# HGRN2 scores: two chunks in one product, half of the scores transposed

## The chip, the cores and the metric

The kernel runs on one core of one Trainium2 chip. The number that counts is the device time in microseconds of one execution, as the median of several. Inside the core, TensorE multiplies matrices into PSUM, VectorE and ScalarE work on elements, GpSimd clears memory and issues some transfers, and SyncE (SP) issues most of the transfers between HBM and the on-chip memory SBUF.

## The reference, cut to what matters

One layer of a decoder trunk over 512 tokens and 1024 channels: a combined projection, four causal mixers side by side, a gated merge, an output projection and an MLP. The change is in mixer A, HGRN2, which has 4 heads with 128 key and 128 value channels:

```
diff = cum[:, :, :, None, :] - cum[:, :, None, :, :]
dec = jnp.exp(jnp.where(causal[:, :, None], diff, NEG_BIG))
a = jnp.einsum('bhtd,bhtsd,bhsd->bhts', q_, dec, k_)
o = (jnp.einsum('bhts,bhsv->bhtv', a, v_)
     + jnp.einsum('bhtd,bhdv->bhtv', q_ * jnp.exp(cum), S))
```

`cum` is the running sum of the log of the forget gate within a chunk. The score of query t and key s is a sum over 128 channels, each with its own decay between s and t. The decay stands inside the sum, so one plain product of queries and keys does not give it. Only s <= t counts.

## The kernel before

Chunks. The kernel takes chunks of 128 tokens, so a head has NCH = 4 chunks, and arrays have the 128 channels in the partitions and 512 tokens in the columns. `A` (tile name `hA`) holds the scores, 128 partitions (keys s) by 4 chunks of 128 columns (queries t).

Levels. A decay between s and t can be split at any point m between them, exp(cum[t] - cum[m]) times exp(cum[m] - cum[s]), and then the sum over channels is a plain product. The kernel does so by levels n = 1, 2, 4, ..., 64: at level n, tokens are cut into blocks of 2n, and the split point is the middle of each block. The scores of queries in a second half with keys in the first half of the same block come from that level. The diagonal comes from q times k, summed over channels by a product with ones. Level 1 is done in the same way (`p1`, `p1d`). For n from 2 on, `level(n)` makes a tile `g` (name `hG`) of 512 columns: decayed keys where a token is in a first half, decayed queries where it is in a second half.

Products. For n = 2, 4, 8, 16, each chunk of `g` is multiplied with itself, four 128x128 fp32 products into one PSUM tile (`hg`), and a predicated copy with mask `h{n}` takes the wanted squares into `A`. For n = 32 and 64, `g` is packed differently (keys of all chunks in one half, queries in the other), two products give everything wanted, and 4 or 2 small copies of n partitions take out the squares. After the levels the head makes `he`, `hqd`, `hkd`, transposes the decayed keys (`hkt`), and runs over the four chunks: scores times values, state times queries, new state (`ho`, `htb`, `hgS`).

Order of the work. Nothing is issued in the order of the source. Every call goes through a recorder (`_Flow`, `wrap`, line 223; matmuls at line 434, transposes at 475), which keeps its engine, a cost by formula, and what it depends on. VectorE's cost is 65 + 1.04 n ns for n elements a partition where a PSUM operand or two inputs are involved (line 214), a ScalarE operation costs 92 + 0.833 n from SBUF, a DMA of SyncE 500 ns. `lay_out` then runs a list schedule over five engines with these costs and writes the instructions of each engine in the resulting order; on the chip each engine follows its order and waits on semaphores. Two kinds of tasks are mixed. The stream is the sequence of the projections: weight loads of 1 MB (`raw`, on SP's queue), the split of each weight into a high and a low part (`whi` on ScalarE, `wlo` on VectorE), and three matmuls of 512 columns for each pair (`pf`, `pt`, `pbr`, `yo`, `dn`). The mixers' heads are the other tasks, up to five at once. On TensorE the stream has the lowest rank:

```
rank = (9 if eng == "pe" and not self.urgent else 0, i)
```

On the other engines it has the highest. The stream's order is: projections of the mixers, then four merges (branches 3, 0, 1, 2; attention is branch 2 and comes last), each in two halves of four gate units (`pf`) and four branch units (`pbr`), then the output projection (`yo`) and the MLP (`pf` from `h_hi`, and `dn`).

Constants are one array in HBM, loaded by `late_constants` into the tile `cm` by one DMA on SP's queue, after the first units are under way: masks `y32`, `y64` (used by mixer D too), `h1` to `h64`, and others.

At the end, the last output tile is scaled and added in two VectorE pieces of 256 columns, each written out by a DMA on SP's queue.

Of the kernel before, what the change touches and what calls it, by code (L numbers as in the profile page):

```python
# [20 lines left out]
P = 128  # L21
# [17 lines left out]
def shape_constants():  # L39
    cols = []  # L40
    pos = 0

    def put(name, a):
        nonlocal pos
        full = np.zeros((P, a.shape[1]), np.float32)
        full[: a.shape[0]] = a
        _OFF[name] = (pos, pos + a.shape[1])
        pos += a.shape[1]
        cols.append(full)

    i = np.arange(P)
    s, t = i[:, None], i[None, :]
    put("ident", np.eye(P))
    put("minc", np.where(t >= s, 0.0, NEG))
    put("mstr", np.where(t > s, 0.0, NEG))

    def first_to_second(a, b, n):
        return (a // (2 * n) == b // (2 * n)) & ((a // n) % 2 == 0) & ((b // n) % 2 == 1)

    for n in (32, 64):  # L60
        put(f"y{n}", (first_to_second(t, s, n)) * 1.0)
    for n in (1, 2, 4, 8, 16, 32, 64):
        put(f"h{n}", first_to_second(s, t, n) * 1.0)
    put("scan", np.tile((np.arange(T) % P != 0) * 1.0, (P, 1)))
    sgn = np.ones((P, 1))
    sgn[32:36] = -1.0
    sgn[64:68] = -1.0
    put("sgn", sgn)
    global NCONST
    NCONST = pos  # L70
    dist = 255 - np.arange(384)
    nf = np.maximum(dist, 16).astype(np.float32)
    large = 16 + (np.log(nf / np.float32(16)) / np.float32(math.log(8.0)) * np.float32(16)).astype(np.int32)
    bucket = np.where(dist < 16, dist, np.minimum(large, 31))
    ok = (dist >= 0) & (dist < 128)
    oneh = np.zeros((33, 384))
    for m in range(384):
        if ok[m]:
            oneh[bucket[m], m] = 1.0
        else:  # L80
            oneh[32, m] = NEG
    put("oneh", oneh)
    return np.concatenate(cols, 1).astype(np.float32)
# [6 lines left out]
class _Flow:  # L90
# [85 lines left out]
    def wrap(self, key, eng):  # L176
        flow = self

        class W:
            def __getattr__(self, name):  # L180
                fn = getattr(eng, name)

                def call(*a, **k):
                    ops = dict(k)
                    if "out" not in ops:
                        ops["out"], a = a[0], a[1:]
                        call_a = (ops["out"],) + a
                    else:
                        call_a = a
                    out = ops.pop("out")  # L190
                    outs = [out] + ([ops.pop("accum_out")] if "accum_out" in ops else [])
                    ins = [v for v in list(a) + list(ops.values()) if isinstance(v, bass.AP)]
                    n = 1
                    for d in out.shape[1:]:
                        n *= d
                    big = [v for v in ins if v.space == PSUM]
                    table, dma = None, 0
                    if name == "dma_start":
                        dma = n * out.shape[0] * 4
                        c = 1000 if key == "g" else 500 if key == "y" else 60  # L200
                    elif key == "v":
                        if name == "tensor_tensor_scan":
                            c = 65 + 2.09 * n
                        elif name == "reciprocal":
                            c = 65 + 6.26 * n
                        elif name in ("tensor_copy", "tensor_scalar", "memset") and not big:
                            c = 65 + 0.52 * n
                        elif name in ("reduce_sum", "reduce_max"):
                            m = 1
                            for d in ins[0].shape[1:]:  # L210
                                m *= d
                            c = 65 + 1.04 * m
                        else:
                            c = 65 + 1.04 * n
                        if name in ("tensor_scalar", "scalar_tensor_tensor") and len(ins) > (1 if name == "tensor_scalar" else 2):
                            c += 65
                    elif key == "s":
                        f = a[1] if name == "activation" and len(a) > 1 else k.get("func")
                        table = {AF.Exp: "e", AF.Ln: "e", AF.Sigmoid: "s", AF.Silu: "u"}.get(f)
                        c = (52 if big else 92) + 0.833 * n + 95 * ("accum_out" in k) + 93 * sum(isinstance(k.get(x), bass.AP) for x in ("scale", "bias"))  # L220
                    else:
                        c = 110 + n * (0.8 if name == "memset" else 2.15 if len(ins) > 1 else 1.0)
                    flow.record(key, c, lambda: fn(*call_a, **k), outs, ins, table, dma,  # L223
                                two="accum_out" in k)

                return call

        return W()
# [176 lines left out]
def tile_hybrid_parallel_gated_mixers(  # L405
# [96 lines left out]
    def con(name):  # L502
        a, b = _OFF[name]
        return cm[:, a:b]

    def con4(name):
        return con(name).unsqueeze(1).to_broadcast([P, NCH, P])
# [653 lines left out]
    def hg_head(h):  # L1161
# [14 lines left out]
        act(p1, p1, AF.Exp)  # L1176
        tt(p1, p1, two[1][:, :, 1], ALU.mult)
        tt(p1, p1, two[2][:, :, 0], ALU.mult)
        p1d = bcast("hd", onesr, parts("hp", p1), ps("hd", (P, 256)))
        V.copy_predicated(A.rearrange("p (c a u) -> p c a u", c=NCH, u=2)[:, :, :, 1],  # L1180
                          con("h1").bitcast(I32).rearrange("p (a u) -> p a u", u=2)[:, :, 1].unsqueeze(1)
                          .to_broadcast([P, NCH, 64]), p1d.rearrange("p (c a) -> p c a", c=NCH))

        def level(n):
            nb = T // (2 * n)

            def four(a):
                return a.rearrange("p (a u n) -> p a u n", u=2, n=n)

            cv = four(cum)  # L1190
            mid = cv[:, :, 0, n - 1:n].to_broadcast([P, nb, n])
            g = z2("hG")
            gv = four(g) if n < 32 else g.rearrange("p (u a n) -> p a u n", u=2, n=n)
            tt(gv[:, :, 0, :], mid, cv[:, :, 0, :], ALU.subtract)
            tt(gv[:, :, 1, :], cv[:, :, 1, :], mid, ALU.subtract)
            act(g, g, AF.Exp)
            tt(gv[:, :, 0, :], gv[:, :, 0, :], four(k)[:, :, 0, :], ALU.mult)
            tt(gv[:, :, 1, :], gv[:, :, 1, :], four(q)[:, :, 1, :], ALU.mult)
            return g

        for n in (2, 4, 8, 16, 32, 64):
            g = level(n)
            yield
            if n < 32:
                gp = bank4("hg", lambda c, o: mm(o, ch(g, c), ch(g, c)))
                V.copy_predicated(c3(A), con4(f"h{n}").bitcast(I32), c3(gp))
                continue

            gp = ps("hg", (P, 2, P))
            for i in range(2):  # L1210
                mm(gp[:, i, :], ch(g, i), ch(g, 2 + i))
            A5 = A.rearrange("p (i c t) -> p c i t", i=2, c=2)
            for b in range(P // n):
                cc, s0 = b // (64 // n), b % (64 // n) * 2 * n
                V.tensor_copy(A5[s0:s0 + n, cc, :, s0 + n:s0 + 2 * n], gp[b * n:(b + 1) * n, :, b * n:(b + 1) * n])
        e = z2("he")
        act(e, cum, AF.Exp)
        qd, kd = z2("hqd"), z2("hkd")
# [456 lines left out]
    def mlp_units():  # L1675

        for hf in range(NH):
# [11 lines left out]
            for j in range(2):  # L1689
                obox = {}  # L1690
                for kg in range(FH // 4):
                    r0 = (hf * FH + kg * 4) * P
                    subs = []
                    for k2 in range(2):
# [5 lines left out]
                        def step(k, c, kg=kg, k2=k2, box=box, obox=obox, hf=hf, j=j, ah=ah, al=al):  # L1700
                            kk = kg * 4 + k2 * 2 + k
                            if kk == 0 and c == 0:
                                obox["o"] = [ps("dn") for _ in range(4)]
                            o = obox["o"][c]
                            mm3(o, ch(ah[kk], c), ch(al[kk], c), box["hi"][:, k, :], box["lo"][:, k, :],
                                kk == 0, kk == FH - 1)
                            n = 2 if kk == FH - 1 and hf == NH - 1 and j == 1 and c == 3 else 1
                            for a in range(n if kk == FH - 1 else 0):
                                cs = slice(a * T // n, (a + 1) * T // n)
                                stt(acc[c][j][:, cs], o[:, cs], tail["rs2"][:, c:c + 1], acc[c][j][:, cs], ALU.mult, ALU.add)  # L1710
                                if hf == NH - 1:
                                    Y.dma_start(out[c * P:(c + 1) * P, j * T + cs.start:j * T + cs.stop], acc[c][j][:, cs])

                        order = [(k, c) for k in range(2) for c in range(4)]
                        if kg == FH // 4 - 1 and k2 == 1:
# [95 lines left out]
```

## Time and profile before

| | |
|---|---|
| median of 3 runs | 1097.21 us (1096.2 to 1097.26) |
| the profiled execution | 1096.43 us |
| its span on the core | 1094.6 us |
| TensorE busy | 1081.7 us, 99% |
| VectorE busy | 678.4 us, 62% |
| ScalarE busy | 535.6 us, 49% |
| granted TensorE clock, mean | 0.997 |

The span runs from the first to the last instruction in the profile; the execution's own time is 1.83 us longer. A matmul's bar ends by a model and overlaps with the next matmul's bar, so its price is read from start to start. PE is TensorE's matmuls, PEld its weight loads, DVE is VectorE, ACT is ScalarE, SPq is SyncE's queue. Almost every line of the trace is line 223, 434 or 475, the recorder's, so instructions are told apart by their tiles.

### The profile page before, as it was taken

To read this page: it belongs to the slowest core of one execution; us is meant where nothing else is said; L and a number is where in the kernel's file an instruction comes from. 1 tells how busy PE (TensorE), PEld (TensorE's weight loads), DVE (VectorE), ACT (ScalarE), POOL (GpSimd) and SP (SyncE) were. 2 spreads that over 40 slices of the span, in tenths; PEclk is the share of its full clock that TensorE was granted. 3 is DMA by queue.
4 is the path that set the end of the run, shared out by engine and by line. 5 is a ranking of instruction groups with operands and counts; after the bars stand their busy time and mean duration, and the time that the engine had idled before them with its cause. 6 is when DMAs were issued, how large, how long until landed. Compare 5 with 4: busy or idle time off the path is not lost.

```text
span 1094.6 us, 14138 instructions
## 1 busy us (share of the span) xinstructions
PE 1081.7 (99%) x5339; PEld 905.9 (83%) x5339; DVE 678.4 (62%) x1417; ACT 535.6 (49%) x970; POOL 30.2 (3%) x69
## 2 busy tenths in 40 slices
PE   8999999999999999999999999999999999999998
PEld 8889888898888888778887888888888888888886
DVE  5765999758999999976387334545443324444232
ACT  5764478226774778776267233345442222443220
POOL 4000000000000001000000010000000000000000
PEclk8999999999999999999999999999999999999999
DMA  6342554515422355222322252323232323232331
GB/s 235 89 107 97 157 182 153 185 49 167 142 87 87 108 170 174 78 78 78 116 78 77 83 186 91 102 77 116 77 116 77 116 77 116 78 115 80 113 116 39
DMA packets 95580, 122.19 MB, mean 112 GB/s; under 512 B 11104, under 2 KB 65844, under 8 KB 95256
## 3 DMA queue, kind: packets, MB, share of 16 engines
q1 hardware_dynamic: 90216, 115.03, 32.3%
q0 software_dynamic: 1984, 5.61, 1.6%
q10 hardware_dynamic: 3312, 0.66, 0.3%
q8 instruction: 42, 0.69, 0.3%
q14 instruction: 26, 0.21, 0.1%
HBM read 110.74 MB, written 12.11 MB: 112 GB/s over the span
## 4 chain that ended last, share of the span: by engine, by line
PE 79%; DVE 12%; ACT 5%; issue 2%; DMA 1%; SPq 0%; DVEq 0%; ACTq 0%
PE pf L434 41%; PE dn L434 16%; PE pbr L434 6%; PE yo L434 4%; PE pt L434 4%; DVE wlo L223 2%; DVE hG L223 2%; DVE hA L223 1%; ACT whi L223 1%; ACT L223 1%; ACT L400 1%; PE dnt L434 1%; DMA raw<-in_w_in_dram 1%; PE yp L434 1%; PE up L434 1%
## 5 line engine op out<-in xcount | busy, mean ns | idle before, releaser
L223 DVE TENSOR_TENSOR wlo<-raw,whi 128x512 fp32r<-128x512 f32 (+1 forms) x340 | 224.1, 686 | 224.9 <-ACT whi L223 224.5
L223 ACT ACTIVATE whi<-raw 128x512 fp32r<-128x512 f32 (+1 forms) x340 | 199.1, 625 | 286.0 <-PE dn L434 121.7
L434 PE MATMUL pf<-hT_lo,whi 128*128 128x512 f32 (+1 forms) x568 | 220.3, 388 | 0.3 <-DVE hT_lo L223 0.3
L434 PE MATMUL pf<-hT_hi,whi 128*128 128x512 f32 (+1 forms) x568 | 219.8, 387 | 0.0
L434 PE MATMUL pf<-hT_hi,wlo 128*128 128x512 f32 (+1 forms) x568 | 219.3, 386 | 0.0
L434 PEld LDWEIGHTS pf<-hT_lo,whi 128*128 128x128 f32 x568 | 107.4, 189 | 19.2 <-DVE hT_lo L223 0.6
L434 PEld LDWEIGHTS pf<-hT_hi,whi 128*128 128x128 f32 x568 | 107.5, 189 | 18.8
L434 PEld LDWEIGHTS pf<-hT_hi,wlo 128*128 128x128 f32 x568 | 107.4, 189 | 18.2
L434 PE MATMUL pf<-h_hi,whi 128*128 128x512 f32 x256 | 99.8, 390 | 0.0
L434 PE MATMUL dn<-whi,uh 128*128 128x512 f32 x256 | 99.6, 389 | 0.0
L434 PE MATMUL dn<-wlo,uh 128*128 128x512 f32 x256 | 99.6, 389 | 0.0
L434 PE MATMUL dn<-whi,ul 128*128 128x512 f32 x256 | 99.6, 389 | 0.0
L434 PE MATMUL pf<-h_hi,wlo 128*128 128x512 f32 x256 | 99.4, 389 | 0.0
L434 PE MATMUL pf<-h_lo,whi 128*128 128x512 f32 x256 | 99.4, 389 | 0.0
L223 DVE TENSOR_SCALAR ur<-pf 128x512 f32<-128x512 f32 x32 | 22.1, 692 | 71.5 <-PE pf L434 71.5
L434 PEld LDWEIGHTS pf<-h_hi,wlo 128*128 128x128 f32 x256 | 48.1, 188 | 10.1
L434 PEld LDWEIGHTS dn<-wlo,uh 128*128 128x128 f32 x256 | 48.1, 188 | 10.0
L434 PEld LDWEIGHTS dn<-whi,ul 128*128 128x128 f32 x256 | 48.1, 188 | 10.0
L434 PEld LDWEIGHTS pf<-h_lo,whi 128*128 128x128 f32 x256 | 48.1, 188 | 9.9
L434 PEld LDWEIGHTS pf<-h_hi,whi 128*128 128x128 f32 x256 | 48.1, 188 | 9.9
L434 PEld LDWEIGHTS dn<-whi,uh 128*128 128x128 f32 x256 | 48.1, 188 | 9.9
L223 ACT ACTIVATE gate<-pf 128x512 f32<-128x512 f32 x32 | 19.2, 601 | 67.0 <-PE pf L434 66.8
(389 smaller groups left out, 1786.3 us busy)
## 6 DMA issues: line engine op xcount, KB each, us to landing
raw<-in_w_in_dram SPq DMA_DIRECT2D x41, 1024.0 KB, 5.0
raw<-in_w_up_dram SPq DMA_DIRECT2D x16, 1024.0 KB, 5.1
raw<-in_w_down_dram SPq DMA_DIRECT2D x16, 1024.0 KB, 4.9
raw<-in_w_branch_dram SPq DMA_DIRECT2D x8, 1024.0 KB, 4.9
raw<-in_w_out_dram SPq DMA_DIRECT2D x4, 1024.0 KB, 4.9
xt<-in_x_dram SPq DMA_DIRECT2D x4, 512.0 KB, 7.4
acc<-in_x_dram POOLq DMA_DIRECT2D x8, 256.0 KB, 4.8
out_dram<-acc SPq DMA_DIRECT2D x7, 256.0 KB, 2.2
```

Of the source, the lines that this page charges most:

```text
L223: flow.record(key, c, lambda: fn(*call_a, **k), outs, ins, table, dma, two="accum_out" in k)
L400: self.nc.scalar.preload_act_table_set("natural_log_exp_and_others")
L434: fl.record("pe", c, lambda: nc.tensor.matmul(o, lhsT, rhs, start=start, stop=stop), [o], [lhsT, rhs], two=rhs.dtype == F32)
```

## The change

At every level from 2 to 64, one product now serves two chunks. Chunks i and 2+i (i = 0, 1) are paired. The keys of a level stay where they are, and the queries of chunk i go to the query columns of chunk 2+i and the other way round. Then `ch(g, i)` holds keys of chunk i and queries of chunk 2+i, and `ch(g, 2 + i)` the keys of chunk 2+i and the queries of chunk i. Their product has the scores of chunk i with keys in rows, and the scores of chunk 2+i with queries in rows, that is transposed. `keep(n, data)` takes the two halves into `A` by two predicated copies of 128 columns each, with mask `h{n}` for chunks 0 and 1 and mask `y{n}`, its transpose, for chunks 2 and 3. Level 1 goes through `keep` too. The packed form for 32 and 64 and its small copies are gone. After the last level, chunks 2 and 3 of `A` are transposed on TensorE (`hAT`) and copied back by ScalarE.

Three more edits come with it. The masks `y1` to `y16` are added to the constants, 640 more columns. The planner's cost of a ScalarE or VectorE operation on 32 to 64 partitions grows by 90 ns. The last output tile is cut into 384 and 128 columns instead of 256 and 256, and the second piece's DMA is issued by ScalarE.

```diff
-    for n in (32, 64):
-        put(f"y{n}", (first_to_second(t, s, n)) * 1.0)
     for n in (1, 2, 4, 8, 16, 32, 64):
         put(f"h{n}", first_to_second(s, t, n) * 1.0)
+        put(f"y{n}", first_to_second(t, s, n) * 1.0)
...
+                    if key in "vs" and not dma and 32 <= out.shape[0] <= 64:
+                        c += 90
...
+    def cols(ap, off, *dims):
+
+        return bass.AP(tensor=ap.tensor, offset=ap.offset + off, ap=[list(ap.ap[0])] + [list(d) for d in dims])
...
+        def keep(n, data):
+
+            for off, msk, at0, d in ((0, f"h{n}", n, data[0]), (256, f"y{n}", 0, data[1])):
+                dst = cols(A, off + at0, (P, 2), (2 * n, 64 // n), (1, n))
+                V.copy_predicated(dst, cols(con(msk), at0, (0, 2), (2 * n, 64 // n), (1, n)).bitcast(I32), d)
+
         p1d = bcast("hd", onesr, parts("hp", p1), ps("hd", (P, 256)))
-        V.copy_predicated(A.rearrange("p (c a u) -> p c a u", c=NCH, u=2)[:, :, :, 1],
-                          con("h1").bitcast(I32).rearrange("p (a u) -> p a u", u=2)[:, :, 1].unsqueeze(1)
-                          .to_broadcast([P, NCH, 64]), p1d.rearrange("p (c a) -> p c a", c=NCH))
+        keep(1, [cols(p1d, P * u, (64, 2), (1, 64), (1, 1)) for u in range(2)])
...
-            g = z2("hG")
-            gv = four(g) if n < 32 else g.rearrange("p (u a n) -> p a u n", u=2, n=n)
-            tt(gv[:, :, 0, :], mid, cv[:, :, 0, :], ALU.subtract)
-            tt(gv[:, :, 1, :], cv[:, :, 1, :], mid, ALU.subtract)
+            def queries(a):
+                return cols(a, n, (256, 2), (2 * n, 128 // n), (1, n))
+
+
+            g, cv = z2("hG"), four(cum)
+            gk, gq = four(g)[:, :, 0, :], cols(g, 256 + n, (-256, 2), (2 * n, 128 // n), (1, n))
+            tt(gk, cv[:, :, 0, n - 1:n].to_broadcast([P, T // (2 * n), n]), cv[:, :, 0, :], ALU.subtract)
+            tt(gq, queries(cum), cols(cum, n - 1, (256, 2), (2 * n, 128 // n), (0, n)), ALU.subtract)
             act(g, g, AF.Exp)
-            tt(gv[:, :, 0, :], gv[:, :, 0, :], four(k)[:, :, 0, :], ALU.mult)
-            tt(gv[:, :, 1, :], gv[:, :, 1, :], four(q)[:, :, 1, :], ALU.mult)
+            tt(gk, gk, four(k)[:, :, 0, :], ALU.mult)
+            tt(gq, gq, queries(q), ALU.mult)
             return g
...
-            if n < 32:
-                gp = bank4("hg", lambda c, o: mm(o, ch(g, c), ch(g, c)))
-                V.copy_predicated(c3(A), con4(f"h{n}").bitcast(I32), c3(gp))
-                continue
-
-            gp = ps("hg", (P, 2, P))
+            gp = ps("hg", (P, 256))
             for i in range(2):
-                mm(gp[:, i, :], ch(g, i), ch(g, 2 + i))
-            A5 = A.rearrange("p (i c t) -> p c i t", i=2, c=2)
-            for b in range(P // n):
-                cc, s0 = b // (64 // n), b % (64 // n) * 2 * n
-                V.tensor_copy(A5[s0:s0 + n, cc, :, s0 + n:s0 + 2 * n], gp[b * n:(b + 1) * n, :, b * n:(b + 1) * n])
+                mm(ch(gp, i), ch(g, i), ch(g, 2 + i))
+            keep(n, [cols(gp, n * (1 - u), (P, 2), (2 * n, 64 // n), (1, n)) for u in range(2)])
+        at_ = ps("hAT", (P, 256))
+        for i in range(2):
+            transpose(ch(at_, i), ch(A, 2 + i))
+        S.copy(A[:, 256:T], at_)
...
-                            n = 2 if kk == FH - 1 and hf == NH - 1 and j == 1 and c == 3 else 1
-                            for a in range(n if kk == FH - 1 else 0):
-                                cs = slice(a * T // n, (a + 1) * T // n)
+                            end = (0, 3 * P, T) if hf == NH - 1 and j == 1 and c == 3 else (0, T)
+                            for a in range(len(end) - 1 if kk == FH - 1 else 0):
+                                cs = slice(end[a], end[a + 1])
...
-                                    Y.dma_start(out[c * P:(c + 1) * P, j * T + cs.start:j * T + cs.stop], acc[c][j][:, cs])
+                                    (S if cs.start else Y).dma_start(
+                                        out[c * P:(c + 1) * P, j * T + cs.start:j * T + cs.stop], acc[c][j][:, cs])
```

## Rows read from the trace of the kernel before

**Rows 1.** The page: engines' busy time, and 40 slices in tenths.

```profile
PE 1081.7 (99%) x5339; PEld 905.9 (83%) x5339; DVE 678.4 (62%) x1417; ACT 535.6 (49%) x970; POOL 30.2 (3%) x69
...
PE   8999999999999999999999999999999999999998
...
PEclk8999999999999999999999999999999999999999
```

**Rows 2.** The chain that ended last: start us, us, what.

```profile
651.70 10.88 PE pbr L434 x48
...
1003.59 87.05 PE dn L434 x384
```

**Rows 3.** Stretches: busy us and count by engine, clock, DMA share, GB/s.

```profile
262.00:383.00 121.00, 120.48 (x682) 101.61 (x680) 116.84 (x280) 83.33 (x135) 2.18 (x11) 1.00 0.36 114
383.00:600.00 217.00, 213.73 (x1047) 173.52 (x1048) 166.57 (x413) 149.52 (x307) 5.46 (x11) 1.00 0.33 107
600.00:1000.00 400.00, 400.00 (x1782) 331.37 (x1781) 172.93 (x269) 141.25 (x252) 4.26 (x8) 1.00 0.31 100
```

**Rows 4.** TensorE's waits: us in total, times, longest.

```profile
PE apt L475 <- DVE aL L223: 2.3, 5, 0.8
```

**Rows 5.** Tile of the branches' low parts: min/median/max ns, first and last start.

```profile
L223 DVE TENSOR_TENSOR brl<-aos,brh x16: 408/420/423, 557.1 to 601.4; 64x256 fp32r<-64x256 f32 x16
```

**Rows 6.** Tile `hg`, the score products.

```profile
L434 PE MATMUL hg<-hG x160: 270/275/348, 276.0 to 367.3; 128*128 128x128 f32 x160
```

**Rows 7.** TensorE's timeline around one group of score products: start us, us.

```profile
353.11 1.05 PE L434 MATMUL hg<-hG 128*128 128x128 f32 x8
353.92 0.48 PE L434 MATMUL ssb<-sqh,onesr 128*128 128x512 f32 x1
354.24 0.39 PE L434 MATMUL pf<-hT_lo,whi 128*128 128x512 f32 x1
```

**Rows 8.** The same around four transposes of decayed keys.

```profile
290.88 0.60 PE L475 MATMUL hkt<-identt,hkd 128*128 128x128 f32 x4
291.24 0.49 PE L434 MATMUL pf<-hT_hi,wlo 128*128 128x512 f32 x1
```

**Rows 9.** A ScalarE copy of 128x256 from PSUM, by its tile.

```profile
L223 ACT COPY akv<-pt x4: 373/374/376, 93.4 to 102.5; 128x256 f32<-128x256 f32 x4
```

**Rows 10.** VectorE's timeline in the HGRN2 stage.

```profile
353.38 0.72 DVE L223 COPY_PREDICATED hA<-cm,hd 128x256 f32<-128x256 int32 x1
353.88 0.46 DVE L223 TENSOR_TENSOR hG<-hx 128x256 f32<-128x256 f32 x1
...
364.14 0.72 DVE L223 COPY_PREDICATED hA<-cm,hg 128x512 f32<-128x512 int32 x1
364.76 0.67 DVE L223 TENSOR_TENSOR hkd<-hx 128x512 f32<-128x512 f32 x1
365.36 1.42 DVE L223 TENSOR_TENSOR hG<-hG,hx 128x256 f32<-128x256 f32 x4
366.70 0.67 DVE L223 TENSOR_TENSOR hkd<-hkd,hx 128x512 f32<-128x512 f32 x1
...
367.97 1.55 DVE L223 COPY hA<-hg 32x64 f32<-32x64 f32 x6
```

**Rows 11.** ScalarE's and VectorE's timelines, writes of 64 partitions in attention.

```profile
555.43 3.95 ACT L223 ACTIVATE brh<-aos 64x256 fp32r<-64x256 f32 x9
...
557.13 2.21 DVE L223 TENSOR_TENSOR brl<-aos,brh 64x256 fp32r<-64x256 f32 x5
```

**Rows 12.** VectorE's timeline, the last two pieces of the output.

```profile
1090.67 0.88 DVE L223 SCALAR_TENSOR_TENSOR acc<-dn,rs,acc 128x256 f32<-128x256 f32 x2 [0.61 <-PE dn L434]
```

**Rows 13.** Stretches of 0.1 us while the last piece is written out.

```profile
1092.60:1092.70 0.10, 0.00 (x0) 0.00 (x0) 0.00 (x0) 0.00 (x0) 0.00 (x0) 1.00 1.09 389
...
1092.90:1093.00 0.10, 0.00 (x0) 0.00 (x0) 0.00 (x0) 0.00 (x0) 0.00 (x0) 1.00 0.17 41
```

**Rows 14.** DMA issues: line engine op, KB each, median us to landing.

```profile
dnU<-dnd ACTq DMA_DIRECT2D x2, 64.0 KB, 2.1
```

More of the change, by code (lines that the diff above doesn't have):

```diff
@@ L1178, in hg_head @@
         tt(p1, p1, two[2][:, :, 0], ALU.mult)
+        def keep(n, data):
+            for off, msk, at0, d in ((0, f"h{n}", n, data[0]), (256, f"y{n}", 0, data[1])):
+                dst = cols(A, off + at0, (P, 2), (2 * n, 64 // n), (1, n))
+                V.copy_predicated(dst, cols(con(msk), at0, (0, 2), (2 * n, 64 // n), (1, n)).bitcast(I32), d)
         p1d = bcast("hd", onesr, parts("hp", p1), ps("hd", (P, 256)))
-        V.copy_predicated(A.rearrange("p (c a u) -> p c a u", c=NCH, u=2)[:, :, :, 1],
-                          con("h1").bitcast(I32).rearrange("p (a u) -> p a u", u=2)[:, :, 1].unsqueeze(1)
-                          .to_broadcast([P, NCH, 64]), p1d.rearrange("p (c a) -> p c a", c=NCH))
+        keep(1, [cols(p1d, P * u, (64, 2), (1, 64), (1, 1)) for u in range(2)])
         def level(n):
-            nb = T // (2 * n)
             def four(a):
                 return a.rearrange("p (a u n) -> p a u n", u=2, n=n)
-            cv = four(cum)
-            mid = cv[:, :, 0, n - 1:n].to_broadcast([P, nb, n])
-            g = z2("hG")
-            gv = four(g) if n < 32 else g.rearrange("p (u a n) -> p a u n", u=2, n=n)
-            tt(gv[:, :, 0, :], mid, cv[:, :, 0, :], ALU.subtract)
-            tt(gv[:, :, 1, :], cv[:, :, 1, :], mid, ALU.subtract)
+            def queries(a):
[4 more added lines that the diff above has]
+            tt(gq, queries(cum), cols(cum, n - 1, (256, 2), (2 * n, 128 // n), (0, n)), ALU.subtract)
             act(g, g, AF.Exp)
-            tt(gv[:, :, 0, :], gv[:, :, 0, :], four(k)[:, :, 0, :], ALU.mult)
-            tt(gv[:, :, 1, :], gv[:, :, 1, :], four(q)[:, :, 1, :], ALU.mult)
+            tt(gk, gk, four(k)[:, :, 0, :], ALU.mult)
+            tt(gq, gq, queries(q), ALU.mult)
             return g
```

## The prediction

> **What bounds the kernel now.** The page comes first. [...] So time goes away only with TensorE work, or with a wait of TensorE. The chain that ended last says the same from the end backwards: its last piece is 384 projection matmuls in 87.05 us, 0.2267 us each, with no other engine between them [rows 2]. A busy bar of one matmul is longer than that (the next starts before its modelled end), so the step from start to start is the price, not the bar.
>
> The stretches show where TensorE loses anything [rows 3]. Between 600 and 1000 us it is idle for nothing. In the stage of the four HGRN2 heads, 262 to 383 us, it is idle for 0.52 us, and from 383 to 600 us, mostly sliding-window attention, for 3.27 us; the largest single kind of wait there is the transpose of the attention weights behind VectorE, 2.3 us in five waits [rows 4]. A late start of under about 0.16 us hides inside the bars, so the true loss is somewhat above these 3.8 us.
>
> Why can TensorE be that full? The projections are filler: their matmuls have the lowest rank in the planned order, so the planner puts one wherever a head is not ready. The filler does not run dry either. The last write of the attention branch starts at 601.4 us [rows 5], and its first reader, the first half of the last merge, starts at 651.70 us [rows 2]. The mixers have 50 us of slack against the stream that needs them. So work taken from TensorE in the HGRN2 stage moves everything behind it forward, unless new waits appear in the written order.
>
> **The change, part by part.** Removed products. At levels 2, 4, 8 and 16 each head makes four 128x128 fp32 products, at 32 and 64 two each: 20 per head. The trace has 160 matmul instructions for them, so 80 products of two instructions [rows 6]. Afterwards each of the six levels has two products, 12 per head. That removes 4 x 8 = 32 products. Price: a run of eight instructions starts at 353.11 and the next matmul at 353.92, 0.81 us; the one after starts 0.32 us later where the step in pure filler is 0.23 [rows 2], so 0.09 us belongs to the run [rows 7]. 0.90 us for four products is 0.225 us each. 32 x 0.225 = 7.2 us.
>
> Added transposes. Two per head bring chunks 2 and 3 back to the right orientation. Four such transposes take 0.36 us to the next start [rows 8], and with the same 0.09 us 0.45, so 0.11 each: 8 x 0.11 = 0.9 us. Net on TensorE: -6.3 us. Its fp32 input and its loads are of the same kind, so I see no other TensorE term.
>
> The hop behind the transposes. ScalarE must copy 128x256 out of PSUM per head; such a copy took 0.37 us [rows 9]. ScalarE is busy 83.33 of 121 us in this stage [rows 3], so 4 x 0.37 = 1.5 us fits there. What is queued behind: the head's products of scores and values, which now wait for transposes and copy, and the filler stands between. The same pattern exists already: at 290.88 four transposes of the decayed keys, then a ScalarE copy, then products, and the filler continues at 291.24 [rows 8]. I cost the hop at nothing; with no filler between, it would be 4 x 0.37 = 1.5 us, plus handovers.
>
> VectorE. Per head it now runs four predicated copies of 512 elements, one strided one of 256, four copies of 32x64 and two of 64x128. Steps to the next start: 0.62 us for the 512 form, 0.50 for the strided 256, and six small copies in 1.55, so 0.26 each [rows 10]. Sum 4 x 0.62 + 0.50 + 6 x 0.26 = 4.5 us. Afterwards: 7 levels x 2 predicated copies of 128 elements, a form that the trace lacks. From rows: 256 more elements of an ordinary operation cost 0.265 us (a step of 0.60 at 512 elements, 1.34 for four at 256), so 1.03 ns each [rows 10]. Then the 512 form has 0.09 fixed, and the strided form costs (0.50 - 0.09)/256 = 1.6 ns an element. For 128 elements: 0.23 dense, 0.30 strided; a price under nothing is excluded, since each is an instruction of its own, and the far upper bound is the whole 0.50 of the strided form. The new patterns have short runs at the low levels and longer ones above, so I take 0.27: 14 x 0.27 = 3.8 us, 0.75 less per head, between 1.3 and 0.3 less at the two nearest prices. VectorE has 4.2 us idle in the stage [rows 3] and gains 3.0; it is not what sets the end, so none of this is in the sum. If that cover went (0.50 each), see the slower rival.
>
> [...]
>
> The planner's 90 ns on ScalarE and VectorE operations of 32 to 64 partitions. Nothing on the chip changes by it but the order that is written. Is it truer? Nine 64x256 ScalarE writes took 3.95 us and five VectorE ones 2.21 us, 0.44 each [rows 11]; the planner's formulas give 0.305 and 0.331. So the planner believed these to be 0.11 to 0.13 short, and attention and mLSTM have many. A truer order should lose some of the waits of [rows 4]. Bounds: it can gain about the TensorE idle of 383 to 600 us, 3.3 us [rows 3], and a newly drawn order can as well lose as much again. I take a third of the 2.3 us of [rows 4]: -0.8 us. This is the weakest term.
>
> The tail. The last tile's two pieces become 384 and 128 columns, and the second leaves by ScalarE's queue. The two VectorE operations take 0.88 us now [rows 12] and together the same afterwards, so the last data is ready at the same time. The last piece, which moved until about 1092.95 at up to 389 GB/s [rows 13], is 64 KB where it was 128: 0.17 us less. The piece ahead of it is 64 KB longer and can stand in its way, so I take -0.1. ScalarE's queue has landed 64 KB in 2.1 us [rows 14], from issue, and the old last piece was moved 1.4 us after the end of its VectorE operation, so I keep +0.3 as the other bound.
>
> Constants. 640 more columns add 320 KB to one load on SP's queue at about 25 us, 0.8 us at that rate; the weight loads are behind it. TensorE has no wait on a weight load in the list of waits after its start and the second to fifth slices are full [rows 1], so nothing; 0.8 if that cover failed.
>
> Sum: -7.2 + 0.9 - 0.8 - 0.1 = -7.2 us. The profiled execution took 1096.43 us (span 1094.6 and 1.83 around it): 1089.2. The median of the runs shown lies 0.78 above it, so 1090.0.
>
> **The rivals.** VectorE's lag hands a part back. The planner prices a 128-element predicated copy at 0.198 us. At 0.30, 56 of them run 5.7 us behind plan. Now the lag of the replaced operations, by its formula, is 16 x 0.02 + 4 x 0.17 + 16 x 0.13 + 8 x 0.06 = 3.6 us. If the 2.1 more and half to all of the hop's 1.5 reach TensorE, and the new order gives nothing: 1090.0 + 2.1 + 0.75 to 1.5 + 0.8, so 1093.6 to 1094.4. For it: VectorE is 97% busy here. Against: the present 3.6 us of lag go with only 0.52 us of TensorE idle.
>
> The truer order gains more: all 3.3 us instead of 0.8, so 1087.5.
>
> Nothing comes of it. The order is written anew with the old tuned constants, and TensorE waits 5.0 to 9.4 us more than I forecast: within 2.2 us of before, 1097.2. For it: waits in a static order cannot be read from the old trace. Against: more than all visible waits of 383 to 600 us again.
>
> Slower. Predicated copies cost by their pattern, not their count: 0.50 each, like the strided one of 256. Then VectorE needs 14 x 0.50 = 7.0 us per head, 2.45 more, 9.8 in all, in a stage that is 6.3 us shorter and had 4.2 idle: 11.9 us over. If all of it held TensorE up: 1090.0 + 11.9 = 1101.9. Against it: later stretches have 50 us of VectorE idle [rows 3] to which head work can slide. It turns the sign where the price passes about 0.42 us (56 x 0.095 more, and the 2.1 by which the stage shrinks past its idle, make 7.4) and nothing slides.
>
> **How the numbers follow.** The forecast, TensorE's saving passing through with waits about as before: 0.60, own range 1088 to 1092. VectorE's lag 0.18 (near 1094), the better order 0.10 (1087.5), nothing 0.07, slower 0.05. The range, 1087.0 to 1094.2, holds the first three and leaves out the last two and the edges, some 0.17. A 0.2% step, 2.2 us, is what a measurement here can tell from no change: faster 0.88, same 0.07, slower 0.05.
>
> **What would show it.** The score products in 96 instructions where there are 160, with the same step of 0.11; eight new transposes; the first matmul of the MLP some 6 to 8 us earlier, with 700 to 1000 us as dense as before. Predicated copies of 128 elements with a step of 0.23 to 0.30. TensorE idle in 262 to 380 us near 0.5 us; above 2 us the lag rival is right. The wait of the attention transposes below 2.3 us, or the planner's term is wrong. The last transfer under 1.5 us behind the last VectorE operation. The prediction fails if the new order places head products where VectorE is late, which shows as TensorE idle behind the predicated copies.

## The result, and the profile after

The change took the median from 1097.24 to 1081.76 us, ratio 0.9866 with a 95% interval of 0.9854 to 0.9878. By that ratio it is 14.7 us off (the two medians lie 15.5 apart), twice the 7.2 that were forecast and outside the range. The profiled execution's span is 1080.0 us where it was 1094.6.

The page of the changed kernel, engines and slices, answers to [rows 1]:

```profile
PE 1068.5 (99%) x5283; PEld 897.4 (83%) x5283; DVE 672.9 (62%) x1429; ACT 531.9 (49%) x972; POOL 30.5 (3%) x69
...
PE   7999999999999999999999999999999999999998
...
PEclk9999999999999999999999999999999999999999
```

The shares look as before, so they do not say where the 14.6 us went. The chain that ended last answers to [rows 2]:

```profile
637.15 10.88 PE pbr L435 x48
...
989.05 87.05 PE dn L435 x384
```

Its last piece is as long as before, to the hundredth, and starts 14.54 us earlier; the last merge starts 14.55 us earlier. So all but 0.1 us came from the time before the last merge. The stretches of [rows 3], in the changed kernel:

```profile
262.00:383.00 121.00, 120.91 (x677) 103.53 (x677) 117.02 (x308) 89.94 (x149) 3.64 (x16) 1.00 0.41 127
383.00:600.00 217.00, 215.92 (x1055) 177.20 (x1054) 163.98 (x403) 143.80 (x303) 3.96 (x6) 1.00 0.32 103
600.00:1000.00 400.00, 400.00 (x1782) 331.27 (x1782) 173.78 (x269) 140.75 (x252) 4.26 (x8) 1.00 0.31 102
```

TensorE's idle time between 262 and 600 us fell from 3.79 to 1.17 us. That is still only 2.6 us. The rest of the lost time is the kind that a busy bar hides. It can be worked out: in dense work every matmul of a shape has a usual step to the next (0.2267 us for 512 columns, 0.120 for 256, 0.126 for 272, 0.1125 for an fp32 instruction of 128), and the listing by shape gives their counts. From 50 to 600 us, taken as one stretch, the counts times these steps fill all but 14.6 us of the 550 before, and all but 8.0 after. (Another profile with the same TensorE order gave 15.7, so differences of about 1 us say nothing. The absolute values hang on the steps that are taken, the difference hardly does.) So TensorE lost 6.6 us less by work that arrives late, beside the saved work of 6.3. At the start, the granted clock, before and then after:

```profile
10.00:12.00 2.00, 2.00 (x10) 2.00 (x11) 1.81 (x5) 1.50 (x3) 0.00 (x0) 0.50 1.01 399
12.00:14.00 2.00, 1.82 (x9) 1.52 (x7) 2.00 (x5) 2.00 (x6) 0.00 (x0) 0.50 1.07 383
```

```profile
10.00:12.00 2.00, 1.56 (x13) 1.09 (x11) 2.00 (x4) 2.00 (x5) 0.00 (x0) 1.00 1.03 393
12.00:14.00 2.00, 1.04 (x5) 0.80 (x6) 2.00 (x6) 2.00 (x7) 0.00 (x0) 1.00 0.97 337
```

The instructions are the same there. Before, TensorE idled from about 6.8 to 9.9 us for the first input tile and then ran at a granted clock of 0.50 until about 16 us; after, the tile came 0.55 us earlier and the clock stayed at 1.00. By counts times steps the first 50 us lost 9.8 us before and 8.2 after, 1.6 less in these two executions. 6.3 + 6.6 + 1.6 + 0.1 = 14.6 us, the difference of the two spans. The 1.6 belongs to this pair of executions and not to the change: the three other executions of the changed kernel had a mean granted clock of 0.998, not 1.000, and took 1081.07 to 1082.41 us, on average no longer than this one. Without it 13.0 us are accounted for.

TensorE's waits in the changed kernel between 24 and 700 us; the attention transposes of [rows 4] are not in the list:

```profile
PE alo L435 <- DVE ak L224: 0.9, 2, 0.5
PE mcp L476 <- DVE dnW L224: 0.8, 1, 0.8
```

The tiles `hg` and `hA`: 96 product instructions where [rows 6] had 160, 56 predicated copies, 8 transposes and 4 copies back:

```profile
L435 PE MATMUL hg<-hG x96: 270/275/348, 275.1 to 357.8; 128*128 128x128 f32 x96
```

```profile
L224 DVE COPY_PREDICATED hA<-cm,hg x48: 278/292/504, 275.8 to 360.0; 128x128 f32<-128x128 int32 x48
...
L224 DVE COPY_PREDICATED hA<-cm,hd x8: 426/445/500, 270.1 to 348.4; 128x128 f32<-128x128 int32 x8
...
L476 PE MATMUL hAT<-identt,hA x8: 272/272/273, 291.8 to 360.6; 128*128 128x128 f32 x8
...
L224 ACT COPY hA<-hAT x4: 353/356/372, 293.5 to 361.4; 128x256 f32<-128x256 f32 x4
```

VectorE's timeline gives the step of the predicated copies, the form that the old trace lacked:

```profile
281.10 0.90 DVE L224 COPY_PREDICATED hA<-cm,hg 128x128 f32<-128x128 int32 x4
281.89 0.42 DVE L224 TENSOR_TENSOR hG<-hG,hx 128x256 f32<-128x256 f32 x1
...
300.96 0.74 DVE L224 COPY_PREDICATED hA<-cm,hd 128x128 f32<-128x128 int32 x2
301.50 0.80 DVE L224 COPY_PREDICATED hA<-cm,hg 128x128 f32<-128x128 int32 x2
302.09 0.45 DVE L224 TENSOR_TENSOR hG<-hG,hx 128x256 f32<-128x256 f32 x1
```

Four take 0.79 us, 0.20 each; in the lines shown those of levels 1 and 2, with runs of one and two elements, take 0.27 and 0.30, and in the whole trace 0.23 to 0.30.

### The profile page after: what moved, and what is told of

It reads as the page before. It is cut to its first block, busy times and chain, and to the rows that moved or that the text cites. A ratio compares the mean times of both kernels' runs of the same rounds, so it can differ in the third digit from the quotient of the medians.

```text
span 1080.0 us, 14030 instructions
## 1 busy us (share of the span) xinstructions
PE 1068.5 (99%) x5283; PEld 897.4 (83%) x5283; DVE 672.9 (62%) x1429; ACT 531.9 (49%) x972; POOL 30.5 (3%) x69
## 4 chain that ended last, share of the span: by engine, by line
PE 81%; DVE 13%; DMA 3%; ACT 2%; issue 1%; SPq 0%; DVEq 0%; ACTq 0%
PE pf L435 42%; PE dn L435 16%; PE pbr L435 7%; PE pt L435 4%; PE yo L435 4%; DVE wlo L224 2%; DVE hG L224 2%; DMA raw<-in_w_in_dram 1%; DVE hA L224 1%; PE dnt L435 1%; PE yp L435 1%; PE up L435 1%; DMA mrr<-mrrd 1%; DVE on L224 1%; PE apt L476 1%
## 5 line engine op out<-in xcount | busy, mean ns | idle before, releaser
L435 PE MATMUL pbr<-brh,whi 128*128 128x512 f32 x128 | 50.4, 394 | 0.0
```

Source lines behind the costliest of these rows:

```text
L435: fl.record("pe", c, lambda: nc.tensor.matmul(o, lhsT, rhs, start=start, stop=stop), [o], [lhsT, rhs], two=rhs.dtype == F32)
```

## The experiments

Three theories stood for the 8 us beyond the saved work. One: the planner's 90 ns, because a truer cost removes waits. Two: the shorter score items themselves. Three: any newly drawn order moves the time by some us, and this draw was lucky. "n90" is the two lines of the diff that add the 90 ns; each experiment on the planner's costs puts the lines shown in front of `flow.record` in the kernel named.

The ratio is against runs of the kernel before on the same chip, whose median was 1096.4 to 1097.2 us; where two kernels ran on different chips, their ratios are compared and not their medians. The last column is the lost time of the section above, 550 us less counts times usual steps, in each kernel's one profile.

| kernel | median us | ratio to before (95%) | TensorE idle 262-383, 383-600 us | lost time 50-600 us |
|---|---|---|---|---|
| before | 1097.24 | 1 | 0.52, 3.27 | 14.6 |
| the change | 1081.76 | 0.9866 (0.9854-0.9878) | 0.09, 1.08 | 8.0 |
| b_plus90 | 1088.32 | 0.9921 (0.9906-0.9936) | 0.00, 1.21 | 7.1 |
| a_no90 | 1085.33 | 0.9893 (0.9878-0.9907) | 0.26, 2.63 | 10.5 |
| b_tail_consts | 1096.05 | 0.9992 (0.9982-1.0001) | 0.36, 3.86 | 15.7 |
| b_redraw | 1100.22 | 1.003 (1.0021-1.004) | 0.42, 5.50 | 19.6 |
| b90_redraw | 1093.18 | 0.997 (0.9957-0.9983) | 0.34, 2.39 | 13.0 |
| b_placebo | 1092.01 | 0.9954 (0.9938-0.9969) | 0.50, 1.38 | 11.0 |
| b_pess | 1091.92 | 0.9956 (0.9941-0.9972) | 0.02, 2.40 | 10.3 |
| b_minus60 | 1101.34 | 1.0039 (1.0025-1.0052) | 1.45, 5.71 | 19.2 |
| a_plus32 | 1089.17 | 0.9941 (0.9921-0.996) | 0.01, 0.68 | 7.6 |
| b90_hA | 1092.83 | 0.997 (0.9958-0.9982) | 0.08, 3.62 | 11.2 |
| a_redraw | 1083.83 | 0.9879 (0.986-0.9898) | 0.00, 1.10 | 8.4 |
| a_pess | 1083.27 | 0.988 (0.9861-0.9899) | 0.00, 1.57 | 7.5 |
| b90_V | 1089.05 | 0.994 (0.9921-0.996) | 0.00, 2.00 | 9.9 |
| b90_S | 1096.87 | 0.9998 (0.9988-1.0008) | 0.51, 4.19 | 16.4 |
| a_130 | 1083.66 | 0.9889 (0.987-0.9909) | 1.42, 1.31 | 8.7 |

In the nine kernels that change only the planner's costs, the lost time moves with the time, to about 2 us or better in each. So what a new order gives or costs shows as TensorE starting its work late.

### The two halves apart

b_plus90, the kernel before with n90 alone:

```diff
+                    if key in "vs" and not dma and 32 <= out.shape[0] <= 64:
+                        c += 90
```

> The kernel before with the planner's 90 ns alone. Theory 1 (the truer cost removes waits): of the 8.3 us that the change gained beyond TensorE's saved work, most of the 6.8 us behind the start comes here: 1090 to 1093 us. Theory 2 (the shorter score items cause fewer waits, the 90 ns does little): 1096 to 1098 us. Theory 3 (any newly drawn order moves the time by some us): anything in 1093 to 1101, without a pattern in the places where it waits.

a_no90, the changed kernel with these two lines taken out:

> The changed kernel without the planner's 90 ns. Theory 1: it loses what the 90 ns gave, 1086 to 1089 us, with waits back in attention. Theory 2: 1081 to 1083 us. Theory 3: 1079 to 1088 us.

Measured by ratio on 1097.2 us: the 90 ns alone is worth 8.7 us, the rest alone 11.7, both 14.7. Both theories had a part, and they overlap by 5.7. On top of the 90 ns, the rest adds 6.0 us, which agrees with TensorE's saved work and the tail, 6.4 us; with intervals of 1 to 2 us on each ratio it does not show that nothing else is in it. The stretch of attention in b_plus90 and its waits:

```profile
383.00:600.00 217.00, 215.79 (x1067) 178.76 (x1066) 169.19 (x417) 141.82 (x302) 5.34 (x11) 1.00 0.32 99
```

```profile
PE mcp L477 <- DVE dnW L225: 0.6, 1, 0.6
PE akp L477 <- DVE akn L225: 0.6, 1, 0.6
PE apt L477 <- DVE aL L225: 0.5, 1, 0.5
```

In the same 217 us TensorE started 1067 matmuls where [rows 3] has 1047. Twenty more are about 4 us of work, but the shown idle fell by 2.1 only: here one sees the late starts inside the bars (by counts times steps the stretch lost 8.7 us before and 4.2 here). In a_no90 the transposes wait again:

```profile
PE apt L474 <- DVE aL L222: 2.3, 3, 1.5
```

### The small edits

b_tail_consts, the kernel before with the masks `y1` to `y16` and the tail:

```diff
+        put(f"y{n}", first_to_second(t, s, n) * 1.0)
...
+                            end = (0, 3 * P, T) if hf == NH - 1 and j == 1 and c == 3 else (0, T)
```

> The kernel before with only the added masks in the constants and the new cut and queue of the last output piece; TensorE's order stays as it was. My sum: -0.1 us, so 1096.9 to 1097.3. [...]

0.9992 with an interval that holds 1: nothing that can be told from no change. Its granted clock fell at the start too (0.59 and 0.55 from 10 to 14 us, where the changed kernel had 1.00), so the layout of the constants does not by itself give the full clock there.

### Truth, length or luck

b_redraw adds 2 ns to every VectorE operation of the kernel before, b90_redraw does so with n90:

```diff
+                    if key == "v":
+                        c += 2
```

> The kernel before with 2 ns added to the planner's cost of every VectorE operation: an order drawn anew with costs that are hardly truer. Theory 3: it moves by 2 us or more in either direction. Theories 1 and 2: within 1 us or so of 1097.2.

> The kernel before with the 90 ns and 2 ns on every VectorE operation: the order with the truer cost, drawn anew. If the truth of the cost makes the gain: 1086 to 1091 us, near 1088.3 again. If the gain of the 90 ns was a lucky draw: it falls back toward 1094 to 1100.

Theory three has its part: 2 ns cost 3.3 us. Much of that is one wait in mixer D, which stands in every order drawn with the 2 ns, here in b_redraw:

```profile
PE yp L436 <- DVE Tm L225: 2.3, 1, 2.3
```

b90_redraw misses what was expected of a true gain: 1093.18 us is above 1091, and 3.3 us are left of the 8.7. But the 2 ns did their harm elsewhere: from 50 to 262 us, with mixer D, the lost time is 5.0 us in b_redraw and 4.8 in b90_redraw, 1.0 in both first draws. From 262 to 600 us the 90 ns takes it from 13.2 to 5.7 in the first draw and from 14.1 to 7.8 in the second. In time, the 90 ns are worth 1.003 - 0.997, 6.6 us, between the two redraws. So it is no luck of one draw.

b_placebo adds 90 ns to 160 operations of attention on all 128 partitions, b_pess 7 ns to every ScalarE and VectorE operation, b_minus60 takes 60 ns off the operations that n90 touches:

```diff
+                    if key in "vs" and not dma and outs[0].name.split("_")[0] in ("aL", "anm", "aes"):
+                        c += 90
```

```diff
+                    if key in "vs" and not dma:
+                        c += 7
```

```diff
+                    if key in "vs" and not dma and 32 <= out.shape[0] <= 64:
+                        c -= 60
```

> The kernel before with 90 ns added to about as many ScalarE and VectorE operations of attention (160) as the edit touches (167), but to ones of all 128 partitions, which the planner prices rightly. If truth makes the gain: no gain, 1095 to 1102 us. If any longer estimate in this stage helps, since a planned slack costs less than a late engine: 1088 to 1092 us.

> The kernel before with 7 ns added to every ScalarE and VectorE operation, 16 us in all, as much as 90 ns on 167 operations. Truth: 1094 to 1100 us, a redraw like another. Longer estimates help wherever they stand: 1088 to 1092 us.

> The kernel before with 60 ns taken off the operations of 32 to 64 partitions, so that the planner errs by 170 to 190 ns where it erred by 110 to 130. Truth: more waits, 1099 to 1106 us, in the stretches from 340 to 600 us. A lucky draw or slack theory without truth: 1093 to 1100 us.

The placebo's operations were priced rightly before (VectorE's of 512 elements have a step of 0.60 us against 0.597 planned, those of 2 elements 0.07 against 0.067). Both longer estimates without truth, or with little of it, gained 5.0 and 4.8 us, about half of the 90 ns; the falser estimate lost 4.3. The stretch of attention in b_minus60 and in b_placebo:

```profile
383.00:600.00 217.00, 211.29 (x1039) 171.10 (x1038) 168.15 (x416) 145.03 (x301) 5.81 (x13) 1.00 0.32 102
```

```profile
383.00:600.00 217.00, 215.62 (x1065) 177.42 (x1065) 168.48 (x411) 153.70 (x310) 5.46 (x11) 1.00 0.33 107
```

In attention the placebo does as well as the 90 ns (1.38 us idle against 1.21). There a longer estimate is enough, wherever it stands. In the HGRN2 stage, where the placebo changes nothing (0.50 us idle, 0.52 before), the 90 ns brings 0.00; but so does b_pess, nearly (0.02). By counts times steps that stage lost 4.2 us before and with the placebo, 1.1 with the 90 ns and 2.0 in b_pess, so length is worth much of it there as well. My theory of truth alone fell; length counts too.

### Which operations

b90_V and b90_S give the 90 ns to one engine alone (the lines shown are b90_V's; b90_S has "s" for "v"), b90_hA to the 24 small copies into the scores alone:

```diff
+                    if key == "v" and not dma and 32 <= out.shape[0] <= 64:
+                        c += 90
```

```diff
+                    if key == "v" and 32 <= out.shape[0] <= 64 and outs[0].name.split("_")[0] == "hA":
+                        c += 90
```

> The kernel before with the 90 ns on VectorE's operations of 32 to 64 partitions alone (110 of the 167). If TensorE's waits come from VectorE being later than planned, as the list of waits names it: most of the 8.4 us, 1088.5 to 1091.

> The kernel before with the 90 ns on ScalarE's 57 operations alone. If VectorE is the late engine: 1094 to 1098. If the two halves share the gain by count: 1093 to 1094.5.

> The kernel before with 90 ns on the 24 small copies into the scores alone, the underpriced operations that the change removes. If they make the TensorE waits of the HGRN2 and mLSTM stretches: 2 to 3 us off, 1093.5 to 1095, and 250 to 400 us denser. If not: 1096 to 1099.

VectorE's 110 operations carry most of the gain, 6.6 us by ratio; ScalarE's 57 carry none by themselves. The 24 copies are worth 3.3 us. The change removes just these, with or without the 90 ns, which can be more than half of the overlap of 5.7. The HGRN2 stage bears this out: it lost 4.2 us before, 1.9 in b90_hA, and 2.0 in a_no90, where the copies are gone and the 90 ns is not there.

### The price of the products, and better versions

a_plus32 makes four products again at levels 2 to 16; nobody reads the added ones:

```diff
-            gp = ps("hg", (P, 256))
+            gp = ps("hg")
             for i in range(2):
                 mm(ch(gp, i), ch(g, i), ch(g, 2 + i))
+                if n < 32:
+                    mm(ch(gp, 2 + i), ch(g, 2 + i), ch(g, i))
```

> The changed kernel with the 32 removed products put back as additional ones whose results nobody reads (levels 2 to 16 make four products again). My sum prices them at 7.2 us: 1088 to 1090 us if the waits stay as they are. If the planner hides them in waits that are there anyway, less: 1084 to 1087.

By ratio it is 8.2 us above the change, with intervals of 1 to 2 us on each; the medians lie 7.4 apart, on two chips, and so do the two profiled spans (1087.4 and 1080.0), with nearly the same lost time. The sum had 7.2.

a_redraw, a_pess and a_130 (130 ns in place of 90) are the changed kernel with the edits above:

> The changed kernel with 2 ns on every VectorE operation, the order drawn anew. The same step cost the kernel before 3.5 us and the 90 ns version 4.9, nearly all of it by a wait near 211 to 250 us in mixer D: 1084 to 1087 with that wait; 1081 to 1083 if the draw avoids it. Above 1088 the gain of the change would be mostly a lucky draw.

> The changed kernel with 7 ns on every ScalarE and VectorE operation. If longer estimates help wherever waits are left (about 4 us behind the start): 1078 to 1081. If the truer cost has already taken what there was: 1081 to 1084.

> The changed kernel with 130 ns in place of 90, nearer to the 0.11 to 0.13 us by which the rows say that these operations were priced short. If more truth gives more: 1079 to 1081.5. If 90 has taken it, a redraw: 1081 to 1085.

All three came out at 1083.3 to 1083.8 us, by ratio 1.4 to 2.5 us above the change, their intervals overlapping with its own. A still longer or truer cost gives nothing more, and the changed kernel's gain stands in redrawn orders. The changed kernel is the fastest that was run. a_no90 was not redrawn.

## Why the prediction was wrong

Removed products: right. 96 instructions, and the 7.2 us measured as 7.4 between the spans and 8.2 by ratio. Added transposes and net work: right; the 6.0 us that the rest adds on top of the 90 ns answer to -6.3 and -0.1.

The hop behind the transposes: right at nothing. No TensorE wait on `ho` stands in the list after.

VectorE: the price was too high. 0.20 to 0.30 us against 0.27, most at 0.20, below my lower price of 0.23 (0.22 by its own working). It was not in the sum. But it turned the lag rival's sign: the planner's 0.198 fits these copies, so 24 operations that it priced some 0.1 us short gave way to 40 that it prices rightly and 16 that it prices some 0.03 to 0.10 short. VectorE's lag behind plan fell by about 2 us where that rival had it grow by 2.1. This is the likeliest reason why the rest alone brings 11.7 us and not 6.4: b90_hA shows the price of the old copies' wrong cost by itself, 3.3 us. The 2 us that are left are no more than what a redraw by 2 ns can move.

The planner's 90 ns, and with it all that a newly written order gives: the step that failed. The mechanism was named rightly, a truer order with fewer waits, and the size was off: -0.8 us, measured -8.7 alone and -3.0 by ratio on top of the new scores. Counted in that second way the 90 ns explains 2.2 of the 7.5 us by which the forecast missed; the other 5.3 came with the new scores, for whose effect on the order the sum had nothing. Either way, TensorE lost 6.6 us less by late work where the sum had 0.8. Two faults lie in it. I bounded the gain by TensorE's shown idle, 3.3 us, though I had written that bars hide late starts; counts times steps would have given 14.6 us lost from 50 to 600 us, and that was the bound to take. And I looked at attention alone, while the 90 ns also reprices the 24 score copies and the operations of mLSTM. The better-order rival had the right direction, with the same wrong bound.

Why are these operations dearer? [rows 10] show it for VectorE: a 512-element predicated copy has a bar of 0.72 us and a step of 0.62, so the next one starts before it ends. The six small copies are four of 32x64 and two of 64x128, listed there as one row. One by one, their bars are 0.20 to 0.29 us and the five steps between them 0.22 to 0.32, and none starts before the one ahead has ended. (To the next start all six take 1.47 us, and not the 1.55 that the prediction divides by six.) Only the operation behind the last one overlaps with it. The price hangs on the neighbours: the same 64x256 operation of `aos` has a step of 0.34 us in the three places where the next one overlaps with it, and 0.42 to 0.46 where the next one follows at once without overlap. What makes it so was not shown.

The tail and the constants: -0.1 us from the start of the last piece of the chain to the end of the span, against -0.1; nothing for the constants.

What stays open: how much of the 90 ns is truth and how much is plain length, since untrue longer costs gained half as much; and the draw itself: in the three orders redrawn by 2 ns it cost 1.4 to 5.4 us by ratio, and the 11.7 us of the rest alone stand on one draw.

## What to carry to other kernels

In a kernel whose order is planned from costs, operations that are priced 0.1 us short can make the bound engine wait, as here 110 of VectorE's did, and these waits hide inside overlapping bars (before, the stretch of attention lost 8.7 us and showed 3.27 as idle): work out the lost time as the stretch less counts times usual steps, and use that as the bound, not the shown idle. Take the stretch whole, since in a listing of short pieces the matmuls at each edge are counted twice. Where an edit changes both work and planning costs, run the halves apart and one or two redrawn orders, before a gain is put down to either. Replacing operations that the plan misprices by ones that it prices rightly may be worth something beside the work that is saved: here 3.3 us by b90_hA, next to 6.3.

## What the runs showed that was not expected

A predicated copy of 128 elements costs a step of 0.20 us (one of 512 had 0.62), and 0.23 to 0.30 where its runs are one or two elements long (the strided one of 256 had 0.50). In these four forms the price follows the element count, and not the pattern alone. And 2 ns on each VectorE operation, which is hardly a change of cost, moved the kernel by 0.3%.
